# Moving factors and scan results of a state-space layer into PSUM, and writing out the order of its steps

## The chip, the core and the metric

The program runs on one core of one Trainium2 chip. Five engines take instructions from queues of their own, each in order: TensorE (PE, the matmuls), VectorE (DVE), ScalarE (ACT), GpSimd (POOL) and SyncE (SP, which here issues all large DMA transfers). An instruction that waits holds up everything behind it on its engine. The metric is the time of one execution on the device in microseconds (us), lower is better; of the kernel before three runs were taken.

## The reference

An encoder trunk of two layers works on one sequence of 512 positions and 1024 channels. Layer 0 mixes with dilated attention, layer 1 with a bidirectional state-space model (S5); each mixer is followed by a SwiGLU network (FFN 0 and FFN 1), and RMS norms stand ahead of all of them. The change lies in layer 1 and in its tables:

```python
def s5_direction(u, a_re, a_im, log_dt, b_re, b_im, c_re, c_im, reverse):
    dt = jnp.exp(log_dt)[:, None]
    mag = jnp.exp(a_re * dt)
    lr, li = mag * jnp.cos(a_im * dt), mag * jnp.sin(a_im * dt)
    ...
    bbr = fr[..., None] * b_re - fi[..., None] * b_im
    bbi = fr[..., None] * b_im + fi[..., None] * b_re
    bur = jnp.einsum('bsgc,gpc->bsgp', u, bbr)
    bui = jnp.einsum('bsgc,gpc->bsgp', u, bbi)
    ...
    _, _, xr, xi = lax.associative_scan(complex_affine_combine, (ar, ai, bur, bui),
                                        reverse=reverse, axis=1)
    return (jnp.einsum('bsgp,gcp->bsgc', xr, c_re) - jnp.einsum('bsgp,gcp->bsgc', xi, c_im))

def s5_mixer(hn, w_in, ..., d_skip, w_glu):
    u = (hn @ w_in).reshape(b, s, SSM_GROUPS, SSM_GROUP_CH)      # 64 groups of 16 channels
    y = d_skip * u + (s5_direction forward) + (s5_direction backward)
    ag = gelu(y) @ w_glu
    return ag[..., :D_MODEL] * sigmoid(ag[..., D_MODEL:])

def swiglu_ffn(hn, w_in, w_out):
    gu = hn @ w_in
    return (silu(gu[..., :FFN_HIDDEN]) * gu[..., FFN_HIDDEN:]) @ w_out
```

## The kernel before

Activations lie with channels on the partitions: a tile is 128 channels by 512 positions in fp32. A product is taken in three passes (high part by high part, low by high, high by low: `gemm_a`, the matmuls of L764), so one 128x512 result over 1024 channels costs 24 matmuls. For each unit of weights ScalarE writes the high part (`whi`, L116) and VectorE, in the SSM stage GpSimd, the low one (`wlo`, L117).

**Tables.** The scan is done in blocks of 8 positions. For each of 8 channel tiles T and each half s of its groups the class `Tables` computes from the parameters: `bb` (L212 to L217 from `elem_b`, VectorE), the input table `Tn` (`elem_in`, VectorE, L419 to L421, through a scratch tile `tm`), the output table `B` (`elem_out`, GpSimd), the phases `ph` (`elem_ph`, GpSimd, six doublings of a geometric series), and `Z` (`elem_z`, ScalarE, copies of `B` and `C`). TensorE then transposes `Tn` in two steps into `tps` (`tr_in`, L449) and multiplies `bb` by `Z` into `eps` (`band`, L458); ScalarE copies both results out (`Tt`, `E`), and DMAs put all tables into DRAM.

This work is cut into pieces that a planner (`Bg`) lays between the matmuls of FFN 0. Each piece has a cost; every k-tile of a product adds credit in proportion to its time, and the next piece is written into the program when the credit reaches half its cost. So the costs set places only: a piece's VectorE instructions stand in VectorE's queue where the program had got to. FFN 0 itself needs VectorE and ScalarE after each pair of products `gps` and `ups` (`evac`): `g` (L1171, VectorE), Silu (L1172, ScalarE), `u` (L1173) and `u*g` (L1175, VectorE), `hh` (L1178, ScalarE), `hl` (L1179, VectorE). Its results turn over five PSUM banks, the tables' over three.

**The SSM stage.** For each T: a product gives `sps` (24 matmuls), VectorE scales it into `u` (L1388), eight DMAs spread `u` by position into `U` (L1392), 64 small matmuls (L1281) give `V` (two banks, one set), `s_scan` turns `V` by the phases (L1299 to L1301), scans (L1306) and turns back (L1311 to L1313, result `xx`), `s_R` copies `xx` to `x` on ScalarE, half of it in reverse (L1323, L1325), 48 matmuls give `yps` (L1346, L1348), and ScalarE applies Gelu. Every second T the results are transposed (`s_tr`) and split for the GLU product. In the steady state the program of one T has: product T, `s_R` of T-3, V and scan of T-2, output of T-3. First halves of four GLU columns (`glu_part`, copied out by ScalarE at L1452) lie between the last steps.

## Time and profile before

| | us |
|---|---|
| median of 3 runs (1647.0 to 1652.1) | 1649.3 |
| profiled execution, its own time | 1651.6 |
| its span | 1649.6 |
| TensorE busy | 1538.5 (93%) |
| VectorE busy | 984.4 (60%) |
| ScalarE busy | 672.1 (41%) |
| GpSimd busy | 530.0 (32%) |

The span is what the trace covers; the execution's time is 2.0 us longer, and the profiled execution was 2.3 us above the median. TensorE is busy for 93% of the span, so what a change can win lies in the 111 us in which it is not, and in the time in which its clock is granted at less than full speed (the row PEclk, in tenths of full speed). FFN 0 lies from about 570 to 1030 us, the parameters' part of the tables in its first 110 us, the tables themselves from 690 on, the SSM stage from 1030 to 1210.

### The profile page before, as it was taken

To read this page: it belongs to the slowest core of one execution; us is meant where nothing else is said; L and a number is where in the kernel's file an instruction comes from. 1 tells how busy PE (TensorE), PEld (TensorE's weight loads), DVE (VectorE), ACT (ScalarE), POOL (GpSimd) and SP (SyncE) were. 2 spreads that over 40 slices of the span, in tenths; PEclk is the share of its full clock that TensorE was granted. 3 is DMA by queue.
4 is the path that set the end of the run, shared out by engine and by line. 5 is a ranking of instruction groups with operands and counts; after the bars stand their busy time and mean duration, and the time that the engine had idled before them with its cause. 6 is when DMAs were issued, how large, how long until landed. Compare 5 with 4: busy or idle time off the path is not lost. (4 is left out here: it accounts for less than half of the span.)

```text
span 1649.6 us, 22660 instructions
## 1 busy us (share of the span) xinstructions
PE 1538.5 (93%) x8428; PEld 1271.4 (77%) x8428; DVE 984.4 (60%) x1701; ACT 672.1 (41%) x1180; POOL 530.0 (32%) x790
## 2 busy tenths in 40 slices
PE   8999999999998899979979989987799999999997
PEld 6977887888896778767767767776678788888886
DVE  6366665666665588876777785567636533433233
ACT  5255454554464432434434443433333333332222
POOL 1022001011111240488889897445403111011010
PEclk9999999999999899999989998989899999999999
DMA  5321232232222133345655544657722333323332
GB/s 181 90 77 52 65 90 64 77 91 63 79 67 62 44 106 89 108 132 147 182 142 160 152 137 141 240 183 225 220 82 85 102 90 102 97 86 105 109 102 64
DMA packets 279180, 185.16 MB, mean 112 GB/s; under 512 B 39936, under 2 KB 261280, under 8 KB 277024
## 3 DMA queue, kind: packets, MB, share of 16 engines
q1 hardware_dynamic: 278640, 183.13, 37.3%
q8 instruction: 66, 1.08, 0.3%
q10 hardware_dynamic: 432, 0.60, 0.1%
q14 instruction: 42, 0.34, 0.1%
HBM read 154.34 MB, written 27.26 MB: 110 GB/s over the span
## 5 line engine op out<-in xcount | busy, mean ns | idle before, releaser
L117 DVE TENSOR_TENSOR wlo<-wraw,whi 128x1024 fp32r<-128x1024 f32 (+1 forms) x232 | 300.3, 1297 | 184.4 <-ACT whi L116 182.1
L116 ACT ACTIVATE whi<-wraw 128x1024 fp32r<-128x1024 f32 x238 | 241.3, 1018 | 247.9 <-PE ops L1572 73.4
L764 PE MATMUL gps<-xhi,whi 128*128 128x512 f32 x792 | 320.4, 405 | 0.0
L764 PE MATMUL gps<-xhi,wlo 128*128 128x512 f32 x792 | 311.4, 393 | 0.9 <-DVE wlo L117 0.9
L764 PE MATMUL gps<-xlo,whi 128*128 128x512 f32 x792 | 311.2, 393 | 0.5 <-DVE xlo L624 0.5
L958 POOL COPY st<-st 32x4 f32<-32x4 f32 x256 | 59.7, 233 | 457.5 <-ACT P L946 337.9
L764 PEld LDWEIGHTS gps<-xhi,wlo 128*128 128x128 f32 x792 | 149.8, 189 | 34.3 <-DVE wlo L117 1.3
L764 PEld LDWEIGHTS gps<-xhi,whi 128*128 128x128 f32 x792 | 150.0, 189 | 28.5 <-issue 2.5
L764 PEld LDWEIGHTS gps<-xlo,whi 128*128 128x128 f32 x792 | 150.3, 190 | 26.4 <-DVE xlo L624 0.8
L764 PE MATMUL ups<-xhi,wlo 128*128 128x512 f32 x352 | 139.6, 397 | 2.0 <-DVE wlo L117 2.0
L764 PE MATMUL ups<-xhi,whi 128*128 128x512 f32 x352 | 140.9, 400 | 0.0
L764 PE MATMUL ups<-xlo,whi 128*128 128x512 f32 x352 | 139.1, 395 | 0.0
L1175 POOL TENSOR_TENSOR u<-u,g 128x512 f32<-128x512 f32 x22 | 28.4, 1291 | 211.3 <-DVE u L1173 202.2
L946 ACT ACTIVATE P<-P,st 128x256 f32<-128x256 f32 x128 | 63.8, 499 | 70.3 <-DVE st L943 70.1
L1172 ACT ACTIVATE g<-g 128x512 f32<-128x512 f32 x44 | 27.8, 632 | 129.9 <-DVE g L1171 129.9
L764 PEld LDWEIGHTS ups<-xhi,wlo 128*128 128x128 f32 x352 | 67.2, 191 | 17.2 <-DVE wlo L117 2.8
L764 PEld LDWEIGHTS ups<-xhi,whi 128*128 128x128 f32 x352 | 67.3, 191 | 14.9 <-issue 1.5
L764 PEld LDWEIGHTS ups<-xlo,whi 128*128 128x128 f32 x352 | 67.2, 191 | 13.6
L866 PE MATMUL vps<-whi,xhi 128*128 128x256 f32 x256 | 73.3, 287 | 0.0
L764 PE MATMUL fps<-hh,whi 128*128 128x512 f32 x176 | 72.7, 413 | 0.0
L1178 ACT ACTIVATE hh<-u 128x512 fp32r<-128x512 f32 x44 | 27.8, 633 | 109.9 <-POOL u L1175 87.4
L866 PE MATMUL vps<-whi,xlo 128*128 128x256 f32 x256 | 72.4, 283 | 0.0
(321 smaller groups left out, 3262.9 us busy)
## 6 DMA issues: line engine op xcount, KB each, us to landing
wraw<-in_w_ffn_in SPq DMA_DIRECT2D x88, 512.0 KB, 3.8
wraw<-in_w_qkv SPq DMA_DIRECT2D x72, 512.0 KB, 3.6
wraw<-in_w_ffn_out SPq DMA_DIRECT2D x38, 512.0 KB, 4.0
BD<-B SPq DMA_DIRECT2D x16, 512.0 KB, 3.5
TinD<-Tt SPq DMA_DIRECT2D x16, 512.0 KB, 2.6
Ti<-TinD SPq DMA_DIRECT2D x8, 1024.0 KB, 6.0
Bt<-BD SPq DMA_DIRECT2D x8, 1024.0 KB, 6.3
wraw<-in_w_attn_out SPq DMA_DIRECT2D x8, 512.0 KB, 3.8
```

Source lines behind the costliest of these rows:

```text
L116: nc.scalar.activation(out=hv, in_=wv, func=ACTF.Copy)
L117: self.lo_engine.tensor_tensor(out=lv, in0=wv, in1=fv(hv), op=ALU.subtract)
L764: nc.tensor.matmul(dst, w[:, kt, :], x, start=(start and kt == ks[0] and j == 0), stop=(stop and kt == ks[-1] and j == 2))
L866: nc.tensor.matmul(ps[rp][:, r % 2, :], x, w[:, kk, :], start=(kt == 0 and j == 0 and r % 2 == 0), stop=(kt == 7 and j == 2 and r % 2 == 1))
L946: nc.scalar.activation(out=Pt[:, j, :], in_=Pt[:, j, :], func=ACTF.Exp, bias=st[:, 32 + off + j:33 + off + j], accum_out=st[:, 8 + off + j ...
L958: nc.gpsimd.tensor_copy(par[32 * z:32 * z + 32, y, :, :], own[32 * y:32 * y + 32, z, :, :])
L1172: nc.scalar.activation(out=g, in_=g, func=ACTF.Silu)
L1175: eng.tensor_tensor(out=u, in0=u, in1=g, op=ALU.mult)
L1178: nc.scalar.activation(out=hi, in_=u, func=ACTF.Copy)
```

## The change

**Tables.** `bb` and the scratch tile `tm` move from SBUF into PSUM (`pbb`, `ptm`, one bank each); a ScalarE copy of `bb` stays in SBUF for TensorE (`bbs`). The banks come from FFN 0's results (five to four) and the tables' results (three to two). The phases become products of two tables of 8 entries, prepared with the parameters (`AB`): six GpSimd operations of 128x512 for each T in place of 36 smaller ones and two memsets. The sign that ScalarE applied to `B` moves into the parameters. `Tn` and `B` get two buffers, and `band` and `tr_in` of a half-table run while the next half-table's elements are under way (`behind`). The planner's costs fall from 528,900 to 384,750 ns in sum, so its ratio to the 321.7 us of FFN 0 goes from 1.68 to 1.22.

**SSM stage.** There are two sets of V banks. `s_scan` is split into `s_pre`, which writes the scans' results back into V's banks, and `s_post`, which reads them there. Transposes go in halves through a bank of half the size, with a copy back to SBUF. The order of all steps is written out in one list, and the first halves of GLU columns (`fill`) are cut in two. The number of matmuls is the same (7696).

```diff
-        bb = self.bb[:, :, 0:128].rearrange("p i (g c) -> p i g c", g=8)
+        self.bbP = bb = self.pbb.tile([P, 2, 8, 16], F32, tag="bb", name="bbP")
         self.cmul(V, bb[:, 0], bb[:, 1], bt[:, 0], bt[:, 1], *f, self.t("bbT", [8, 16]))
+        nc.scalar.activation(out=self.bbs[T % 2][:, :, 0:128], in_=bb.rearrange("p i g c -> p i (g c)"), func=ACTF.Copy)
...
-        t, o = self.t("tm", [4, 8, 16]), self.Tn[:, i]
+        t, o = self.ptm.tile([P, 4, 8, 16], F32, tag="tm", name="tm"), self.Tn[T, s][:, i]
         tt(out=o, in0=self.bc(self.pin, 0, g0), in1=self.ch(bb[:, i]), op=ALU.mult)
         tt(out=t, in0=self.bc(self.pin, 1, g0), in1=self.ch(bb[:, 1 - i]), op=ALU.mult)
         tt(out=o, in0=o, in1=t, op=(ALU.subtract, ALU.add)[i])
...
+        sh = [P, 8, 8, 8]
+        lo = [self.AB[:, j, :, 0, 8 * T:8 * T + 8].rearrange("p k (g o) -> p g o k", o=1).to_broadcast(sh) for j in range(2)]
+        hi = [self.AB[:, j, :, 1, 8 * T:8 * T + 8].rearrange("p k (g o) -> p g k o", o=1).to_broadcast(sh) for j in range(2)]
...
+        tt(out=o, in0=hi[0], in1=lo[i], op=ALU.mult)
+        tt(out=t, in0=hi[1], in1=lo[1 - i], op=ALU.mult)
+        tt(out=o, in0=o, in1=t, op=(ALU.subtract, ALU.add)[i])
...
-        if i == 1:
-            nc.scalar.activation(out=B[:, 1], in_=B[:, 1], func=ACTF.Copy, scale=-1.0)
...
-        r = [(3400, lambda i=i: some(i)) for i in range(0, len(ops), n)]
+        r = [(1750, lambda i=i: some(i)) for i in range(0, len(ops), n)]
...
+                behind = [(1600, lambda T=T, s=s: self.band(T, s)), (400, lambda T=T, s=s: self.store_e(T, s)),
+                          (1600, lambda T=T, s=s: self.tr_in(T, s, 0)), (1600, lambda T=T, s=s: self.tr_in(T, s, 1)),
+                          (400, lambda T=T, s=s: self.store_in(T, s))]
...
-                psf = Cycle(((psg, "g"),) * 2 + ((f0.enter_context(tc.tile_pool(name="psf", bufs=3, space=PSUM)), "f"),) * 3)
-                psb = f0.enter_context(tc.tile_pool(name="psb", bufs=3, space=PSUM))
+                psf = Cycle(((psg, "g"),) * 2 + ((f0.enter_context(tc.tile_pool(name="psf", bufs=2, space=PSUM)), "f"),) * 2)
+                psb = f0.enter_context(tc.tile_pool(name="psb", bufs=2, space=PSUM))
+                tabs.ptm = f0.enter_context(tc.tile_pool(name="ptm", bufs=1, space=PSUM))
+                tabs.pbb = f0.enter_context(tc.tile_pool(name="pbb", bufs=1, space=PSUM))
...
-        pV = s0.enter_context(tc.tile_pool(name="psV", bufs=1, space=PSUM))
-        pY = s0.enter_context(tc.tile_pool(name="psY", bufs=2, space=PSUM))
+        pV = s0.enter_context(tc.tile_pool(name="psV", bufs=2, space=PSUM))
+        pY = s0.enter_context(tc.tile_pool(name="psY", bufs=1, space=PSUM))
...
-            for i in range(2):
-                q = W[i]
-                nc.vector.tensor_tensor_scan(out=q, data0=rho, data1=W[i], initial=0.0, op0=ALU.mult, op1=ALU.add)
-                Q.append(q)
+            for q, w in zip((Vr, Vi), W):
+                nc.vector.tensor_tensor_scan(out=q, data0=rho, data1=w, initial=0.0, op0=ALU.mult, op1=ALU.add)
+
+        def s_post(T):
...
+            Q = [vt[T][:, i].rearrange("p g j -> p (g j)") for i in range(2)]
...
+        def s_tr(t2, half):
...
+            for l in range(4):
+                nc.tensor.transpose(yt[:, l], y[:, l], ident)
+            nc.scalar.activation(out=y, in_=yt, func=ACTF.Copy)
+            if half == 1:
...
+        run((s_su, 2), (s_move, 2), (s_g, 3, 0), (s_V, 0), (s_g, 3, 1), (s_su, 3), (s_post, 0), (s_V, 1), (s_g, 4),
+            (s_ph, 0), (s_R, 0), (s_O, 0), (s_su, 4), (s_post, 1), (s_V, 2),
+            (s_g, 5, 0), (s_ph, 1), (s_g, 5, 1), (s_R, 1), (s_O, 1), (s_su, 5), (s_post, 2), (s_V, 3),
+            (s_tr, 0, 0), (s_ph, 2), (s_g, 6, 0), (s_tr, 0, 1), (s_R, 2), (s_post, 3), (s_g, 6, 1), (s_su, 6), (s_V, 4),
+            (s_O, 2), (s_ph, 3), (s_R, 3), (s_post, 4), (s_g, 7, 0), (s_O, 3), (s_g, 7, 1), (s_su, 7), (s_V, 5),
+            (s_tr, 1, 0), (s_ph, 4), (s_tr, 1, 1), (s_R, 4), (s_O, 4), (s_post, 5), (s_V, 6),
+            (next, fill[0]), (s_ph, 5), (next, fill[0]), (s_R, 5), (s_O, 5), (s_post, 6), (s_V, 7), (s_tr, 2, 0),
+            (next, fill[1]), (s_tr, 2, 1), (s_R, 6), (s_post, 7), (next, fill[1]), (s_O, 6), (next, fill[2]), (next, fill[2]))
         ws.lo_engine = nc.vector
-        glu_part(LATE[3])
...
+        run((s_R, 7), (s_O, 7), (next, fill[3]), (s_tr, 3, 0), (next, fill[3]), (s_tr, 3, 1))
```

What this does to the queues is seen at three places. First VectorE around the second half-table of a T, before. `Tn` of the first line is made in two threes (real and imaginary part), `g` to `hl` are the `evac` of one pair of products, `E` the end of the band before.

```order
L463 SCALAR_TENSOR_TENSOR E_6599<-cst_66,dcol_5495,E_6599 128x16
L419 TENSOR_TENSOR Tn_6633<-pin_5565,bb_6378 128x512
L420 TENSOR_TENSOR tm_6634<-pin_5565,bb_6378 128x512
L421 TENSOR_TENSOR Tn_6633<-Tn_6633,tm_6634 128x512
L1171 TENSOR_TENSOR g_6638<-gps2_6532,rsB2_5860 128x512
L1173 TENSOR_TENSOR u_6639<-ups_6576,rsB2_5860 128x512
L1175 TENSOR_TENSOR u_6639<-u_6639,g_6638 128x512
L1179 TENSOR_TENSOR hl_6645<-u_6639,hh_6644 128x512
L117 TENSOR_TENSOR wlo_6652<-wraw_6577,whi_6651 128x1024
L419 TENSOR_TENSOR Tn_6633<-pin_5565,bb_6378 128x512
L420 TENSOR_TENSOR tm_6661<-pin_5565,bb_6378 128x512
L421 TENSOR_TENSOR Tn_6633<-Tn_6633,tm_6661 128x512
```

After, at the corresponding place: the second three of a `Tn`, then the next T's `bb` in PSUM, then an `evac`.

```order
L440 TENSOR_TENSOR Tn_6535<-pin_5566,bbP_6327 128x512
L441 TENSOR_TENSOR tm_6556<-pin_5566,bbP_6327 128x512
L442 TENSOR_TENSOR Tn_6535<-Tn_6535,tm_6556 128x512
L213 TENSOR_TENSOR bbP_6581<-bt_6350,ff_5565 128x128
L214 TENSOR_TENSOR bbT_6582<-bt_6350,ff_5565 128x128
L215 TENSOR_TENSOR bbP_6581<-bbP_6581,bbT_6582 128x128
L216 TENSOR_TENSOR bbP_6581<-bt_6350,ff_5565 128x128
L217 TENSOR_TENSOR bbT_6582<-bt_6350,ff_5565 128x128
L218 TENSOR_TENSOR bbP_6581<-bbP_6581,bbT_6582 128x128
L1195 TENSOR_TENSOR g_6593<-gps2_6486,rsB2_5870 128x512
L1197 TENSOR_TENSOR u_6594<-ups_6540,rsB2_5870 128x512
L1199 TENSOR_TENSOR u_6594<-u_6594,g_6593 128x512
```

The second three of `Tn` stood behind a whole `evac` and a `wlo` before; now it stands ahead of the `evac`, which has the three and six `bb` operations in front of it. The transposes of this `Tn` come only after the following band.

Second, ScalarE at the same places, before: `Z` is filled behind the `evac`'s Silu (`g`), `hh` and `whi`, and the sign of `B` between its two parts.

```order
L461 ACTIVATE E_6599<-eps_6590 128x240
L1172 ACTIVATE g_6638<-g_6638 128x512
L1178 ACTIVATE hh_6644<-u_6639 128x512
L116 ACTIVATE whi_6651<-wraw_6577 128x1024
L438 ACTIVATE Z_6376<-B_6616 64x4x112
L439 ACTIVATE Z_6376<-B_6616 64x4x112
L440 ACTIVATE Z_6376<-C_6383 128x4x16
L116 ACTIVATE whi_6710<-wraw_6649 128x1024
L436 ACTIVATE B_6616<-B_6616 128x512
L438 ACTIVATE Z_6376<-B_6616 64x4x112
L439 ACTIVATE Z_6376<-B_6616 64x4x112
L440 ACTIVATE Z_6376<-C_6383 128x4x16
```

After: copies of `C` and of `bb` come first, then Silu, `hh` and `whi`, then both parts of `Z`.

```order
L116 ACTIVATE whi_6543<-wraw_6487 128x1024
L401 ACTIVATE C_6579<-cps_6576 128x256
L431 ACTIVATE bb1_6319<-bbP_6581 128x2x128
L1196 ACTIVATE g_6593<-g_6593 128x512
L1202 ACTIVATE hh_6599<-u_6594 128x512
L116 ACTIVATE whi_6606<-wraw_6541 128x1024
L459 ACTIVATE Z_6316<-B_6453 64x4x112
L460 ACTIVATE Z_6316<-B_6453 64x4x112
L461 ACTIVATE Z_6316<-C_6325 128x4x16
L459 ACTIVATE Z_6316<-B_6453 64x4x112
L460 ACTIVATE Z_6316<-B_6453 64x4x112
L461 ACTIVATE Z_6316<-C_6325 128x4x16
```

The copy `bb1` waits for VectorE's `bb`, the Silu for VectorE's `g`, and all of `Z`, for which TensorE's next instruction of the tables (`eps`) waits, stands behind both. In the program of before the transposes `tps` came between `Z` and `eps`.

Third, VectorE in the SSM stage, from the turn of one V to the turn of the next, before.

```order
L1299 TENSOR_TENSOR t1_9943<-V_9910,ph_9489 128x512
L1300 TENSOR_TENSOR t2_9944<-V_9910,ph_9489 128x512
L1299 TENSOR_TENSOR t1_9948<-V_9910,ph_9489 128x512
L1300 TENSOR_TENSOR t2_9949<-V_9910,ph_9489 128x512
L1306 SCALAR_TENSOR_TENSOR t1_9943<-rr0_9756,t1_9943 128x512
L1306 SCALAR_TENSOR_TENSOR t1_9948<-rr0_9756,t1_9948 128x512
L1311 TENSOR_TENSOR xx_9955<-t1_9943,ph_9489 128x512
L1312 TENSOR_TENSOR t2_9956<-t1_9948,ph_9489 128x512
L1311 TENSOR_TENSOR xx_9960<-t1_9948,ph_9489 128x512
L1312 TENSOR_TENSOR t2_9961<-t1_9943,ph_9489 128x512
L1388 TENSOR_TENSOR u_10004<-sps2_9967,rsB2_9851 128x512
L1299 TENSOR_TENSOR t1_10040<-V_10007,ph_9609 128x512
```

After, the same stretch: the scans write to `V`, and the scaled `u` of the next product stands between them and the turn back.

```order
L1322 TENSOR_TENSOR t1_9701<-V_9666,ph_9224 128x512
L1323 TENSOR_TENSOR t2_9702<-V_9666,ph_9224 128x512
L1322 TENSOR_TENSOR t1_9706<-V_9666,ph_9224 128x512
L1323 TENSOR_TENSOR t2_9707<-V_9666,ph_9224 128x512
L1327 SCALAR_TENSOR_TENSOR V_9666<-rr0_9493,t1_9701 128x512
L1327 SCALAR_TENSOR_TENSOR V_9666<-rr0_9493,t1_9706 128x512
L1423 TENSOR_TENSOR u_9725<-sps2_9652,rsB2_9588 128x512
L1338 TENSOR_TENSOR xx_9727<-V_9666,ph_9224 128x512
L1339 TENSOR_TENSOR t2_9728<-V_9666,ph_9224 128x512
L1338 TENSOR_TENSOR xx_9732<-V_9666,ph_9224 128x512
L1339 TENSOR_TENSOR t2_9733<-V_9666,ph_9224 128x512
L1322 TENSOR_TENSOR t1_9773<-V_9738,ph_9344 128x512
```

The count is the same; operands move from `t1` (SBUF) to `V` (PSUM), and one `u` goes ahead of the turn back.

## Rows read from the trace of the kernel before

**Rows 1.** Stages: length, busy us of PE, PEld, DVE, ACT, POOL, clock, DMA share, GB/s.

```profile
570.00:690.00 120.00, 115.14 (x510) 93.55 (x509) 102.24 (x198) 38.62 (x49) 30.30 (x23) 1.00 0.36 96
690.00:1030.00 340.00, 301.05 (x1485) 233.70 (x1484) 249.89 (x283) 145.98 (x255) 291.94 (x402) 0.94 0.52 149
1030.00:1078.00 48.00, 43.31 (x196) 34.92 (x194) 23.14 (x37) 21.72 (x21) 19.29 (x11) 1.00 0.64 220
1078.00:1210.00 132.00, 107.28 (x1163) 90.06 (x1163) 83.81 (x93) 47.70 (x70) 62.92 (x40) 0.90 0.65 202
```

**Rows 2.** TensorE's waits, 690 to 1030 us: total, times, longest.

```profile
PE tps L449 <- DVE Tn L421: 38.2, 16, 6.4
PE eps L458 <- ACT Z L440: 0.7, 2, 0.5
```

**Rows 3.** TensorE's waits, 1078 to 1210 us.

```profile
PE yps L1348 <- ACT x L1325: 15.0, 11, 4.8
PE pe L764 <- ACT gpart L1452: 8.9, 1, 8.9
PE V L1281 <- DMA U<-u: 3.5, 1, 3.5
```

**Rows 4.** A matmul's price, from the chain that ended last: start, us, 528 matmuls.

```profile
1521.26 119.69 PE ops L1572 x528
```

**Rows 5.** Groups of VectorE, 690 to 1030 us: count, busy us, mean ns, idle before.

```profile
L420 DVE TENSOR_TENSOR tm<-pin,bb 128x512 f32<-128x512 f32 x32 | 33.4, 1044 | 0.0
L419 DVE TENSOR_TENSOR Tn<-pin,bb 128x512 f32<-128x512 f32 x31 | 28.8, 931 | 0.0
L421 DVE TENSOR_TENSOR Tn<-Tn,tm 128x512 f32<-128x512 f32 x32 | 27.1, 846 | 1.1
```

**Rows 6.** Timeline at 980 us, steps of one evac: start, us, instruction.

```profile
980.10 0.68 DVE L1171 TENSOR_TENSOR g<-gps,rsB 128x512 f32<-128x512 f32 x1
...
980.81 0.63 ACT L1172 ACTIVATE g<-g 128x512 f32<-128x512 f32 x1 [9.26 <-DVE g L1171]
...
981.47 0.74 DVE L1175 TENSOR_TENSOR u<-u,g 128x512 f32<-128x512 f32 x1
...
982.24 0.63 ACT L1178 ACTIVATE hh<-u 128x512 fp32r<-128x512 f32 x1 [0.81 <-DVE u L1175]
```

**Rows 7.** GpSimd's work on the phases (tile ph), 690 to 1030 us.

```profile
690.00:1030.00 340.00, 154.59 (x304) 0.94 0.52 149
```

**Rows 8.** Timeline of the SSM stage, 1104 to 1106 us.

```profile
1104.31 2.08 PE L1281 MATMUL V<-U,Ti 128*64 128x64 f32 x64
...
1104.42 1.28 POOL L1313 TENSOR_TENSOR xx<-xx,t 128x512 f32<-128x512 f32 x1 [0.72 <-PE sps L764]
...
1105.73 0.63 ACT L1323 ACTIVATE x<-xx 64x512 f32<-64x512 f32 x1 [0.72 <-POOL xx L1313]
```

**Rows 9.** Groups of ScalarE, 690 to 1030 us.

```profile
L116 ACT ACTIVATE whi<-wraw 128x1024 fp32r<-128x1024 f32 x40 | 42.0, 1051 | 27.6 <-DMA wraw<-in_w_ffn_in 16.1 <-PE gps L764 6.1 <-PE fps L764 2.8
...
L439 ACT ACTIVATE Z<-B 64x448 f32<-64x448 f32 x31 | 17.8, 575 | 0.4
...
L1172 ACT ACTIVATE g<-g 128x512 f32<-128x512 f32 x15 | 9.5, 632 | 58.5 <-DVE g L1171 58.5
L440 ACT ACTIVATE Z<-C 128x64 f32<-128x64 f32 x31 | 8.0, 257 | 0.5
```

**Rows 10.** VectorE in the parameters' part: their helper's line L178, then everything.

```profile
575.00:680.00 105.00, 34.32 (x114) 1.00 0.36 100
...
575.00:680.00 105.00, 89.12 (x185) 1.00 0.36 100
```

**Rows 11.** Groups of VectorE, 1078 to 1210 us.

```profile
L1306 DVE TENSOR_TENSOR_SCAN t<-rr,t 128x512 f32<-128x512 f32 x16 | 26.8, 1712 | 9.7 <-ACT rr L1287 5.1 <-POOL t L1301 4.6
...
L1299 DVE TENSOR_TENSOR t<-V,ph 128x512 f32<-128x512 f32 x16 | 10.9, 683 | 19.0 <-DMA ph<-PhD 14.8 <-PE V L1281 4.2
...
L1311 DVE TENSOR_TENSOR xx<-t,ph 128x512 f32<-128x512 f32 x16 | 10.7, 669 | 0.0
```

More of the change, by code (lines that the diff above doesn't have):

```diff
@@ L245, in sincos @@
         V = self.V
[L246 removed]
+        sc = [self.scratch(f"sc{i}", 512) for i in range(4)]
+        k_, r, y2, p = (t[:, 0:448] for t in sc)
         two_pi = 2.0 * np.pi
@@ L1384, in build, with s_V, s_O, s_ph @@
+        def s_V(T):
+            s_rho(T)
+            for g in range(8):
+                s_v(T, g)
+            if T + 2 < KT:
+                load_tab(T + 2, "Ti")
+            s_pre(T)
+        def s_O(T):
+            for q in range(4):
+                s_out(T, q)
+            s_gelu(T)
+            if T + 3 < KT:
+                s_move(T + 3)
+            if T + 2 < KT:
+                load_tab(T + 2, "Mt", "Bt")
+        def s_ph(T):
+            load_tab(T + 2, "ph")
         us = {}
```

302 lines of the change are left out of this document (123 added, 179 removed).

## Prediction

> **What bounds the kernel now.** I read the busy time by stage first, then TensorE's waits in the two stages that the change touches, then the groups of VectorE and ScalarE there. The reader is to see in the stages [rows 1] that TensorE sets the time but loses some of it in two places. From 690 to 1030 us, where the tables are built under FFN 0, it is idle for 340 - 301.05 = 39.0 us, and the granted clock is 0.94 of full speed: 0.06 x 340 = 20.4 us at most. From 1078 to 1210 us, the SSM stage, it is idle for 24.7 us, and the clock of 0.90 costs at most 13.2 us. In the stretches between them, where TensorE is busy for 90% or more, the clock is 1.00 [rows 1]; so I read the low clock as what follows the waits, and let its loss go with them in proportion.
>
> The waits have names. In the table stage 38.2 of the 39 us are transposes `tps` that wait for VectorE's `Tn`, 16 times, once for each half-table, and `eps` waits for hardly anything, 0.7 us [rows 2]. In the SSM stage `yps` waits 15.0 us for ScalarE's copies `x`, a GLU product 8.9 us for its bank to be copied out, V 3.5 us for the DMAs into U [rows 3]; with 0.2 us of small ones 27.6 us. The number of matmuls does not change, so nothing else can be won, and about 97 us (39 + 20.4 + 24.7 + 13.2) bounds the gain.
>
> A unit for what follows: 528 matmuls took 119.69 us [rows 4], 0.227 us each. A product over 1024 channels (24) is 5.44 us, a pair of products 10.9 us.
>
> **Table stage, the wait that goes.** From the order and 0.227 us a matmul, `Tn`'s second three stood 5.4 us of TensorE's time ahead of its transposes before, mostly behind a whole `evac`; now it is 9.3 to 11.7 us, because `band` and other pieces come between. The waits of before were 2.4 us in the mean and 6.4 at most [rows 2], and 4 to 6 us more cover them nearly all. I leave 3 us of 38.2.
>
> VectorE gets lighter too. The three operations of `Tn` take 931, 1044 and 846 ns [rows 5]; `g`, as large but with an operand in PSUM, takes 0.68 us [rows 6]. If all three come down to that, 32 x (2.82 - 2.04) = 25 us of VectorE's 249.9 go; if the move to PSUM does nothing, none. No row shows VectorE writing to PSUM; the nearest rows lie at 0.68 (reading it) and 1.04 us, and I take 0.7 to 0.8. GpSimd's phases, 154.6 us in 304 instructions [rows 7], become 48 of 128x512, each about 1.28 us by the nearest row [rows 8], or 61 us. GpSimd isn't waited for, so this counts only by freeing VectorE.
>
> Here a rule of the Trainium skill can be set beside the rows ("SBUF — State Buffer", section "Who interferes with whom"): a VectorE instruction with two SBUF inputs takes an interface that GpSimd's reads share, one with a single SBUF input doesn't. The trace agrees as far as it goes, 0.68 us against 0.85 to 1.04. By it all of `Tn` would run at 0.68 us whatever GpSimd does, but the products in `bb`, with both inputs in SBUF, would be held up as before; the next step's wait would then be nearer to its lower figure, and the sum, with 8 us of waits less and the clock's share, some 12 us lower, 1584.
>
> **Table stage, the wait that comes.** `eps` needs both parts of `Z`, and now it comes 2.8 us of TensorE's time after the second part is issued, with nothing else of the tables between. On ScalarE `Z` stands behind Silu, `hh` and `whi` of an `evac`, and Silu waits for VectorE's `g`, behind `Tn` and the six `bb`. From the end of a pair of products: `g` 0.68, Silu 0.63, `u*g` 0.74, `hh` 0.63 [rows 6], `whi` 1.05, twice (2 x 0.575 + 0.257) for `Z` [rows 9]; 3.7 us to the end of `whi`, 6.5 to that of `Z`. If the end of the pair falls evenly over the 10.9 us ahead of `eps`, and VectorE is on time, the mean wait is 0.36 us: 1.2 us in the 2.2 us in which it falls between the parts of Z, 0.8 in the 1.6 us before. If VectorE is 2 us late it is 1.2 us, if it is 4.2 us late (58.5/14, Silu's mean wait in [rows 9]) 2.6 us. Only 15 pairs, 163 of the 301 us, lie in the stage; the rest are products without `evac`. So 8.7 of the 16 half-tables pay: 3, 11 or 23 us. I take 11, since VectorE has nine operations (6 or 7 us) just ahead of some `g` and none ahead of others.
>
> Banks: with two for `tps`, `eps` and `cps`, the third in a row needs ScalarE's copy of the first. Where an `evac` lies between, I count 0.7 us, four times: 3 us. With four banks for the results a pair's bank is wanted again 10.9 us after it was full, more than the 9.26 us that Silu waited in the rows at 980 us [rows 6], so I put that at nothing; its price if VectorE is later than that is the excess. The sign of `B` that leaves ScalarE and the copy of `bb` that comes there balance.
>
> Waits: 3 + 11 + 3 = 17 in place of 38.9 us, 22 saved; the clock's 20.4 shrink to 20.4 x 17/38.9 = 8.9, 11.5 saved.
>
> **The parameters.** 114 instructions of the helper's line took 34.3 us, 0.30 each [rows 10]; 134 take 40. By the order the first `cps` stands 13 us of TensorE's time earlier, 92 in place of 105 us; the other 54.8 us of VectorE's work there scale to 48, so VectorE is busy for 88 of 92 us. I charge 3 us of waits (0 to 6). The table part gains 22 + 11.5 - 3 = 30 us, between 12 (`eps` at 23) and 43 (`eps` at 3).
>
> **SSM stage.** From V's last matmul the turn takes four products at 0.68, an addition of 1.28 on GpSimd and two scans at 1.7 [rows 8, 11], with the first addition beside the products 6 to 7 us; the turn back, the addition and the copies at 0.63 that the first output matmuls need, 5 more. That is 11 to 12 us. Before, the next product (5.4) and V itself, in the one set of banks, lay in between. In the new order TensorE has, between V of T and its output: 10.2 us for T = 0 (2.7 + V 2.0 + 5.4), 14 to 19 for T = 1 to 3, about 14 for T = 4, 6 and 7, 11 for T = 5. So output 0 waits 0.9, outputs 1 to 3 nothing. The later ones have the time, but ScalarE's queue brings others ahead of `x`: the half-transposes' copies and the high parts, which wait for transposes just ahead of the output (T = 4 and 6: 3.2 and 1.7 us), and copies of `gpart` (T = 5 and 7: 2.3 each). V 0 and 1 still wait 1.6 of the 3.5 us for U. Together 12.0 in place of 27.6 us: 15.6 saved, and of the clock's 13.2 the share 7.5. The scans that write to PSUM have no row; by the nearest, products that read it (683 ns beside 669 from SBUF [rows 11]), nothing is lost; if each of 16 took one more product's time, 0.68 us, most of the 11 us would fall under TensorE's work, and I keep 8 as the bad end. The SSM part gains 23 us, 8 to 33.
>
> **Sum.** 30 + 23 = 53 us. The profiled execution took 1651.6 us, 2.3 above the median of 1649.3, so it would come to 1598.6 and the median to 1596 us.
>
> **Rivals.** (a) The new waits don't come: three waits of some 2 us are left in each stage, and the clock is back at 1.00. Table part 34 + 20 - 3 = 51, SSM part 23 + 13 = 36; 87 us, 1562. For it: the stretches with 96% busy run at full clock [rows 1]. Against it: two queues that have to be on time at once.
>
> (b) The wait only changes its name: VectorE stays as late as it was, since `bb` still reads SBUF, and `eps` pays what `tps` paid. The table part loses its 3 us, SSM gains 23: 1629. For it: VectorE is busy for 249.9 of 340 us [rows 1], and the pairs of products hold more than their share of that.
>
> (c) The transfers take the SSM gain. DMA is busy for 0.65 of 132 us there [rows 1], 86 us, which would be 79% of a stage of 109 us. VectorE waited 14.8 us for `ph` [rows 11]; if that comes onto TensorE's path, SSM keeps 8 us: 38 in all, 1611.
>
> (d) Slower: `eps` takes over the whole of Silu's mean wait in every half-table, 16 x 4.2 = 67 us, with 6 of the others 73 in place of 38.9; the clock follows (+18) and the 3 us, so the tables lose 55, SSM gains 23: 32 slower, 1681. It decides from 3.3 us a half-table on, where the loss is 23. For it: ScalarE's copies of Z have the last place in both queues. Against: half of the half-tables see no `evac`.
>
> **Chances.** The forecast 0.52 (its own range 1576 to 1622), (a) 0.15, (b) 0.11, (c) 0.13, (d) 0.09, of which a third ends within 0.3%, about what a measurement of this kernel can tell from no change. So faster 0.91, same 0.03, slower 0.06. The range of 1558 to 1638 takes in (a) to (c) and leaves out (d) and what lies below (a).
>
> **What would show it.** In the profile after, TensorE's waits from 690 to 1030 us should name `eps` and ScalarE's `Z` with 5 to 20 us and `tps` with under 5; the three operations of `Tn` should take 0.7 to 0.8 us; the clock should be about 0.97 there. In the SSM stage `yps` should wait under 12 us and the GLU product for nothing. It would be wrong if `tps` still waited over 15 us, if new waits for a result bank (`gps`, `ups`) turned up, or if the time came from stretches outside 570 to 1210 us.

## The result

The change makes the kernel slower: 1668.2 us (median of 4 runs, 1662.6 to 1671.3) against 1648.2 us of the kernel before on the same chip (median of 4), a ratio of 1.012 [1.010, 1.014]. The forecast was 1596 us with a range of 1558 to 1638, so it failed in sign and size. The best version of the study keeps the table part and turns two of its steps round: 1618.2 us, a ratio of 0.981 [0.979, 0.983].

### The profile page after: what moved, and what is told of

Same layout as the page of the kernel before. It is cut to its first block, busy times and chain, and to the rows that moved or that the text cites. A ratio compares the mean times of both kernels' runs of the same rounds, so it can differ in the third digit from the quotient of the medians.

```text
span 1669.0 us, 22457 instructions
## 1 busy us (share of the span) xinstructions
PE 1546.2 (93%) x8428; PEld 1273.9 (76%) x8428; DVE 977.7 (59%) x1721; ACT 667.6 (40%) x1180; POOL 449.9 (27%) x535
## 5 line engine op out<-in xcount | busy, mean ns | idle before, releaser
L117 DVE TENSOR_TENSOR wlo<-wraw,whi 128x1024 fp32r<-128x1024 f32 (+1 forms) x232 | 310.9, 1342 | 203.1 <-ACT whi L116 199.7
L452 POOL TENSOR_TENSOR B<-pout,C 128x512 f32<-128x512 f32 x32 | 42.3, 1323 | 155.8 <-DVE pout L178 63.6
L786 PEld LDWEIGHTS ups<-xhi,whi 128*128 128x128 f32 x352 | 66.4, 189 | 14.8 <-issue 1.9
L888 PE MATMUL vps<-wlo,xhi 128*128 128x256 f32 x256 | 72.5, 283 | 0.0
L888 PE MATMUL vps<-whi,xlo 128*128 128x256 f32 x256 | 72.5, 283 | 0.0
```

Source lines behind the costliest of these rows:

```text
L117: self.lo_engine.tensor_tensor(out=lv, in0=wv, in1=fv(hv), op=ALU.subtract)
L452: tt(out=B[:, i], in0=self.bc(self.pout, i, g0), in1=self.ch(C[:, 0]), op=ALU.mult)
L786: nc.tensor.matmul(dst, w[:, kt, :], x, start=(start and kt == ks[0] and j == 0), stop=(stop and kt == ks[-1] and j == 2))
L888: nc.tensor.matmul(ps[rp][:, r % 2, :], x, w[:, kk, :], start=(kt == 0 and j == 0 and r % 2 == 0), stop=(kt == 7 and j == 2 and r % 2 == 1))
```

## The profile after

The profiled execution took 1671.3 us with a span of 1669.0, 19.4 us more than the span before. The first place to look is where these microseconds lie. The table takes them from the first and last matmul of each name in the two traces. 48 matmuls of `pe`, early parts of GLU products, moved from the SSM stage to the GLU columns; their 48 x 0.227 = 10.9 us [rows 4] are counted in both stretches, before and after alike. By its matmuls FFN 0 lies from 595.7 to 1055.9 us before, a little later than the stages suggest.

| stretch | before, us | after, us | difference | forecast |
|---|---|---|---|---|
| FFN 0 with the tables (first `gps` to last `fps`) | 460.2 | 447.3 | -12.9 | -30 |
| SSM stage (to the first `pg`, new order + 10.9) | 161.0 | 165.9 | +4.9 | -23 |
| GLU columns (`pg`, as 288 matmuls) | 65.5 | 93.0 | +27.5 | 0 |

Three differences of -12.9, +4.9 and +27.5 make +19.5, as much as the 19.4 of the spans; what lies ahead of FFN 0 and behind the columns differs by a few us each way and cancels. One trace fixes the first two only to several us. In the seven kernels of the study whose FFN 0 is the changed one it took 447.3 to 454.8 us, in the three with the old one 457.1 to 460.2, so the tables gained some 8 us there. The new SSM order took 162.5 to 167.6 us in five kernels that share it, and these two ends are kernels that differ only behind it. The columns took 93.0 and 93.4 us in the two kernels that have them in this form. So each part has its own answer, and the largest stands where the prediction had not looked. First, the stages, in the columns of [rows 1], after, and the GLU columns before:

```profile
570.00:690.00 120.00, 106.98 (x466) 84.58 (x464) 100.54 (x209) 33.52 (x43) 29.95 (x26) 1.00 0.31 85
690.00:1030.00 340.00, 315.13 (x1582) 244.65 (x1582) 245.04 (x296) 146.18 (x259) 213.44 (x147) 0.97 0.57 163
1078.00:1210.00 132.00, 104.59 (x1026) 87.53 (x1025) 82.87 (x90) 55.93 (x82) 58.79 (x37) 0.88 0.62 202
1210.00:1285.00 75.00, 61.72 (x239) 49.40 (x238) 34.81 (x35) 17.51 (x22) 14.23 (x11) 0.89 0.25 71
```

```profile
1210.00:1285.00 75.00, 72.51 (x324) 59.55 (x322) 47.58 (x48) 26.11 (x32) 19.61 (x15) 1.00 0.29 84
```

In the table stage TensorE is idle for 24.9 instead of 39.0 us, where 17 were forecast; its clock is 0.97 instead of 0.94, as forecast. But from 570 to 690 it is idle for 13.0 instead of 4.9 us, in the SSM window for 27.4 instead of 24.7, and in the GLU columns, where before it was busy for 72.5 of 75 us at full clock, for 13.3 us at a clock of 0.89.

TensorE's waits over the whole span after, as in [rows 2, 3] (total, times, longest):

```profile
PE eps L479 <- ACT Z L461: 21.5, 16, 4.8
PE pg L786 <- DVE gpart L1493: 17.6, 4, 4.7
PE yps L1375 <- ACT x L1352: 14.5, 10, 4.2
PE V L1305 <- DMA U<-u: 8.1, 2, 5.9
PE eps L479 <- POOL tm L413: 7.4, 1, 7.4
```

`tps` is gone from the list (38.2 us before). `eps` takes 28.9 us in its place, `yps` stays near what it was, V waits for U more than twice as long, and a wait of 17.6 us is new: the GLU product `pg` waits for VectorE's addition. Here is one of its four cases, on VectorE and on TensorE (start, us, instruction):

```profile
1249.05 2.20 DVE L117 TENSOR_TENSOR wlo<-wraw,whi 128x1024 fp32r<-128x1024 f32 x1
1251.17 0.68 DVE L1493 TENSOR_TENSOR gpart<-pg,gpart 128x512 f32<-128x512 f32 x1
```

```profile
1251.90 0.50 PE L786 MATMUL pg<-yh,whi 128*128 128x512 f32 x1 [3.95 <-DVE gpart L1493]
...
1252.99 0.63 PE L786 MATMUL pg<-yh,whi 128*128 128x512 f32 x1
1253.42 0.63 PE L786 MATMUL pg<-yl,whi 128*128 128x512 f32 x1
...
1256.35 0.40 PE L786 MATMUL pg<-yh,whi 128*128 128x512 f32 x1
1256.59 0.39 PE L786 MATMUL pg<-yl,whi 128*128 128x512 f32 x1
```

The change does this in lines that the cuts shown above leave out:

```diff
+            pp = pV.tile([P, 2, 8, 64], F32, tag="V", name="pg").rearrange("p i g j -> p i (g j)")
+            pp = [pp[:, i] for i in range(2)]
...
-                    ps = (pY, p1)[part].tile([P, S], F32, tag="yf"[part], name="pg")
```

Both halves of a column now lie in one tile of two banks of V's set, and the addition of the first half is written between the two products. The second product writes to the same tile, so the program makes its first matmul wait for that addition, which stands behind a `wlo` of 2.2 us on VectorE. After the 3.95 us without work the matmuls start 0.43 us apart, which is the clock's lower level (1.2 GHz; the granted clock of 1251 to 1256 us is 0.66), and from 1255.88 on 0.24 us apart again (2.4 GHz). Before, the addition was written at the same place, but each half had a tile of its own, so nothing waited for it, and both additions ran back to back behind both products:

```profile
1255.69 1.27 DVE L1495 TENSOR_TENSOR gpart<-pg,gpart 128x512 f32<-128x512 f32 x2
```

## Experiments

All ratios are to the kernel before on the same chip, with a 95% interval.

### 1. Where the loss lies: the additions, the table part, the SSM part

**GLU additions behind both products** (changed kernel):

```diff
                 for part in range(2):
                     gemm_a(Yl[4:], pp[part], ...)
+                for part in range(2):
                     t = parts.pop((m, part))
```

> The changed kernel with one edit: in the last four GLU columns both halves' products are issued before the two additions, not each addition right behind its product. Theory (the second product waits for the addition of the first, because both write one two-bank tile): the four waits of 17.6 us on the addition go, and with them the low clock of that stretch (8.6 us); 1668 - 26 = 1642 us. Rival A (only the waits go, the low clock has another cause): 1668 - 18 = 1650 us. Rival B (the wait is for a bank set that is still in use from the column two before): nothing changes, 1668 us.

Measured: 1649.5 us, 0.9998 [0.998, 1.0015]. The columns take 65.6 us at full clock: the whole 27.5 us are gone from them. About 20 came back in all, since 7.4 turned up at the first product of FFN 1, which wants the banks of V's set in which the last column lies:

```profile
PE gps L786 <- DVE gpart L1494: 7.4, 1, 7.4
```

**The kernel before with the table part alone**, that is, all edits ahead of the SSM stage:

```diff
+        self.bbP = bb = self.pbb.tile([P, 2, 8, 16], F32, tag="bb", name="bbP")
...
+                tabs.pbb = f0.enter_context(tc.tile_pool(name="pbb", bufs=1, space=PSUM))
```

> The kernel before with the table part of the change alone (class of tables, planner costs, banks under FFN 0); SSM stage and GLU as before. Theory (the parts add up; between the same matmuls the tables gained 29 us after the first half of FFN 0's hidden columns and lost 17 in it): 1648 - 12 = 1636 us. Rival A (as predicted, 30 us gain): 1618 us. Rival B (the gain is lost again in the SSM stage, whose transfers start at another time): 1648 us.

Measured: 1638.8 us, 0.993 [0.990, 0.996].

**The kernel before with the SSM and GLU part alone:**

```diff
+        pV = s0.enter_context(tc.tile_pool(name="psV", bufs=2, space=PSUM))
...
+        run((s_su, 2), (s_move, 2), (s_g, 3, 0), (s_V, 0), ...
```

> The kernel before with the SSM and GLU part of the change alone, the tables as before. Theory: the stage from the last product of FFN 0 to the end of the GLU columns took 32 us longer in the changed kernel, whatever the tables do: 1648 + 32 = 1680 us. Rival A (the loss comes from the tables' new schedule, which leaves transfers behind): 1648 us or less. Rival B (as predicted): 1625 us.

Measured: 1678.6 us, 1.017 [1.014, 1.020].

**The same with the additions behind both products** (first diff):

> The same kernel with the additions of the last four GLU columns behind both products. Theory: 26 us of the 32 are the GLU columns, the SSM steps themselves lose some 5: 1653 us. Rival (the written-out order gains its 23 us once the GLU columns no longer hide it): 1625 us.

Measured: 1658.1 us, 1.005 [1.004, 1.007]. The additions are worth 20.5 us here, and the same 7.4 us are left at FFN 1. The parts add up: 0.7% gained by the tables and 1.7% lost by the rest make 1.0% lost, 1.2% measured. What remains of the SSM order without its GLU columns is worth nothing, not 23 us.

### 2. The tables: who holds `Z`

**ScalarE's copy of `bb` behind `Z`** (table part alone):

```diff
-        nc.scalar.activation(out=self.bbs[T % 2][:, :, 0:128], in_=bb...)
...
+                if s == 1 and T + 1 < KT:
+                    u.append((0, self.copy_b))
```

> The table part alone, with ScalarE's copy of bb moved behind both parts of Z in its queue (where the next T's factors are made). Theory (that copy waits for VectorE, 41.3 us in 6 waits, and holds up Z, for which TensorE waits): the waits of eps in the half-tables behind a bb, some 13 of 26 us, go, with a share of the low clock; 1639 - 15 = 1624 us. Rival (Z is held up as much by the Silu in front of it, which waits for the same VectorE queue): unchanged, 1639 us.

Measured: 1623.3 us, 0.986 [0.984, 0.988].

**An empty piece of 16,000 ns in the planner ahead of the first tables** (table part alone):

```diff
+        r.append((16000, lambda: None))
         r.append((1000, lambda: (self.elem_C(0), self.elem_b(0))))
```

> The table part alone, with an empty piece of 16000 ns cost ahead of the first table, so that the first factors stand 13 us of matmul time later, about where they stood before. Theory (the loss in the first half of the hidden columns is VectorE and GpSimd being late with the parameters at the start): the first wait of eps, 7.3 us, goes; 1639 - 8 = 1631 us. Rival (the loss is in waits of every half-table, and the pause packs the rest 4% closer): 1639 us or a little more.

Measured: 1633.6 us, 0.992 [0.990, 0.994], within the interval of the table part alone. In the trace the first wait of `eps` falls from 7.3 to 3.5 us and FFN 0 from 448.2 to 443.3 us, no more than traces of one FFN 0 differ by.

**`Z` ahead of the next T's `bb`** (table part alone):

```diff
+                u += [(2600, lambda T=T, s=s: self.elem_z(T, s, 0)), (2600, lambda T=T, s=s: self.elem_z(T, s, 1))]
                 if s == 1 and T + 1 < KT:
                     u.append((1500, lambda T=T: (self.elem_C(T + 1), self.elem_b(T + 1))))
-                u += [(2600, lambda T=T, s=s: self.elem_z(T, s, 0)), (2600, lambda T=T, s=s: self.elem_z(T, s, 1))]
```

> The table part alone, with Z's two pieces placed ahead of the next T's factors bb in the planner's list (VectorE's bb then stands behind, not between Tn and the evac of the products). Theory (Z is held up by the copy of bb and by the Silu whose g stands behind bb): the eps waits shrink by as much as with the copy moved, and by the second wait of 6.5 us too; 1623 - 5 = 1618 us. Rival (bb then comes late for the next Tn, and tps waits instead): 1625 us or more.

Measured: 1618.2 us, 0.981 [0.979, 0.983], the best of the study. TensorE's waits for the tables in the table part alone, and with `Z` first:

```profile
PE eps L479 <- ACT Z L461: 18.7, 16, 4.6
PE eps L479 <- POOL tm L413: 7.3, 1, 7.3
```

```profile
PE eps L479 <- POOL tm L413: 7.4, 1, 7.4
PE eps L479 <- ACT Z L461: 4.6, 7, 1.2
...
PE tps L470 <- ACT E L482: 2.4, 2, 1.8
```

The wait for `Z` falls by 14 us, and FFN 0 with the tables takes 429.7 us, 30.5 less than before. That is the gain the prediction had put on the table part.

**The same with an empty piece of 10,000 ns** (as above):

> The same with an empty piece of 10000 ns ahead of the first table. Theory (the first eps still waits 7 us for GpSimd, whose output table waits for VectorE's last parameters): 1618 - 6 = 1612 us. Rival (the pause only moves the wait, as in the run with the pause alone): 1618 us.

Measured: 1621.1 us, 0.984 [0.981, 0.986]. The first wait stays (8.6 us, now on GpSimd's `B`).

### 3. The SSM stage: what is late at `yps`

**Low parts of the weights on VectorE** (changed kernel with the additions behind, as the next three):

```diff
-        ws.lo_engine = nc.gpsimd
+        ws.lo_engine = nc.vector
```

> The changed kernel with the GLU additions behind both products, and with the low parts of the weights made on VectorE, not on GpSimd, in the SSM stage. Theory (five of 16 scans take 3.1 to 3.6 us in place of 1.2, each beside one of GpSimd's low parts, and hold up the outputs' inputs): the scans' total falls from 38.7 to 28 us, 11 low parts of 1.2 us come to VectorE, and the waits of yps fall from 16.6 to about 10; 1649 - 6 = 1643 us. Rival A (the scans are not on the path, the transfers are): 1649 us. Rival B (the low parts in VectorE's queue wait for ScalarE and hold up the turns): 1655 us.

Measured: 1653.0 us, 1.002 [1.000, 1.004]. The sixteen scans get shorter as expected, 28.2 us in sum instead of 36.3, but the stage does not (164.3 instead of 164.8 us), so they are not what it waits for.

**Weight loads issued behind U and `ph`:**

```diff
+                ws.la = 2 if T in (5, 6, 7) else 3
...
+        def s_ld():
+            ws.la = 3
+            ws.load_to(ws.n + 2)
```

> The changed kernel with the GLU additions behind both products, and with the first three loads of GLU weights (8 DMAs each) issued behind the moves into U and the loads of the phases, not ahead of them. Theory (SyncE's queue: the weights' DMAs wait for earlier large transfers and hold up U and ph behind them): the waits of V for U fall from 7.8 to 2 us and VectorE's waits for ph from 27 to about 15, the SSM stage is 9 us shorter; 1640 us. Rival (the transfers themselves are slow, or the weights are late instead): 1649 us or more.

Measured: 1653.6 us, 1.004 [1.002, 1.006]. V's wait for U goes, and two others pay:

```profile
PE yps L1375 <- ACT x L1352: 22.4, 11, 8.9
PE yt L1388 <- ACT ys L1380: 7.2, 1, 7.2
```

**Weight loads of the GLU product from GpSimd's queue:**

```diff
-                    nc.sync.dma_start(
+                    nc.gpsimd.dma_start(
```

> The changed kernel with the GLU additions behind both products, and with the split loads of GLU weights (8 DMAs a unit) issued from GpSimd's queue instead of SyncE's. Theory (SyncE's queue bounds the SSM stage: eight moves into U take it 6 to 9 us, eight loads of weights 6, tables 2, some 16 us for each of 8 T, as long as the stage itself): with the weights gone from it, V's waits for U (7.8 us) and VectorE's for ph (27 us) mostly go, and the stage is 10 to 15 us shorter; 1649 - 12 = 1637 us. Rival A (the transfers, not their issue, are the limit): 1649 us. Rival B (issuing costs GpSimd so much that the additions of the turns come late): 1655 us or more.

Measured: 1648.9 us, 1.000 [0.998, 1.002].

**The moves into U from T = 3 on out of GpSimd's queue:**

```diff
-                nc.sync.dma_start(out=Us[T % 3]...
+                (nc.gpsimd if T > 2 else nc.sync).dma_start(out=Us[T % 3]...
```

> The changed kernel with the GLU additions behind both products, and with the moves into U of T = 3 to 7 (40 DMAs) issued from GpSimd's queue. Theory (SyncE's queue bounds the stage): as in the run with the weights, but the moves stand in GpSimd's order between the turns' additions; 1649 - 10 = 1639 us. Rival A (the transfers are the limit): 1649 us. Rival B (GpSimd's queue, waiting for the output of T before the moves, holds up the turns): 1655 us or more.

Measured: 1645.8 us, 0.998 [0.996, 1.000]. VectorE's wait for `ph` falls from 26.6 to 3.3 us, `yps` still waits 15.4.

**The GLU weights from GpSimd's queue in the old order** (table part with the copy behind `Z`; the diff is that of two runs above):

> The table part with ScalarE's copy of bb behind Z, the SSM stage of before, and the split loads of GLU weights issued from GpSimd's queue. Theory (the 9 us that a GLU product waits are really a weight load that lands late because SyncE issued it late; ScalarE stands idle for 14 us before that unit's high part): that wait goes; 1623 - 10 = 1613 us. Rival A (it is the copy of gpart that is late): 1623 us. Rival B (issuing costs GpSimd too much): 1630 us or more.

Measured: 1636.6 us, 0.992 [0.990, 0.994], some 11 us worse by the ratios than without it: VectorE's scans now wait 18.9 us for GpSimd's additions, behind the issues on its queue.

**All repairs on the changed kernel** (additions, copy of `bb` behind `Z`, and the last GLU column in banks outside V's set):

```diff
+            if m == KT - 1:
+                pp = [pY.tile([P, S], F32, tag="y", name="pg"), pT.tile([P, S], F32, tag="yt", name="pg")]
```

> The changed kernel with three edits: the GLU additions behind both products, the last GLU column's products in two banks outside V's, ScalarE's copy of bb behind Z. Theory (the next product after the GLU columns waits 7.4 us because its banks are those of V's sets, still being read): that wait goes, and 12 to 13 us of the tables as in the run of the tables alone; 1649 - 7 - 12 = 1630 us. Rival (FFN 1's first product waits for the last column's own chain anyway): 1637 us.

Measured: 1628.8 us, 0.987 [0.985, 0.990]. The 7.4 us at FFN 1 are gone.

**The same without the loads of the phases from T = 2 on** (this run and the next leave out transfers that the result needs, so they only price them):

```diff
-            load_tab(T + 2, "ph")
+            ld[T + 2]["ph"] = ld[T % 2]["ph"]
```

> The changed kernel with the three edits, and with the phases of T = 2 to 7 not loaded in the SSM stage (the tables of T = 0 and 1 are used in their place, so six transfers of 512 KB and VectorE's waits for them are left out of the computation). Theory A (VectorE's 25 us of waits for the phases make the turn of V late, 23 us from V to the copies in place of the 11 to 12 predicted): yps waits fall from 16 to under 8 us, the stage is 8 to 12 us shorter; 1629 - 10 = 1619 us. Theory B (ScalarE's queue makes the copies late whatever VectorE does): 1629 us.

Measured: 1618.9 us, 0.983 [0.981, 0.986].

**Also without the moves into U from T = 3 on:**

```diff
-            if T + 3 < KT:
-                s_move(T + 3)
```

> The same, and also without the moves into U for T = 3 to 7 (40 DMAs; old U is used). Theory A (SyncE's queue and the transfers behind it are what the written-out order runs into): V's waits of 7 us go too, and the stage comes near the predicted order, some 20 us shorter than with both: 1629 - 19 = 1610 us. Theory B (ScalarE's queue): at most the 7 us of U, 1622 us.

Measured: 1613.0 us, 0.979 [0.977, 0.981]. By the ratios the two kinds of transfers cost 7 and 8 us, each within some 5. TensorE's wait here, without either:

```profile
PE yps L1381 <- ACT x L1358: 14.5, 11, 3.4
```

**All repairs, `Z` first, phases loaded from GpSimd's queue** (behind its last addition of the same T; nothing is left out):

```diff
-                nc.sync.dma_start(out=t, in_=src)
+                (nc.gpsimd if n == "ph" and T > 1 else nc.sync).dma_start(out=t, in_=src)
```

> The changed kernel with the GLU additions behind both products, the last GLU column in two banks outside V's, Z ahead of the next factors, and the phases of T = 2 to 7 issued from GpSimd's queue right behind the last addition that uses the old ones (nothing is left out). Theory (the phases come late because SyncE reaches them late, not because the transfer is long): VectorE's waits for them go from 25 to under 8 us, 8 of the 10 us that leaving them out gave; 1623 - 8 = 1615 us. Rival (the transfer itself, shared with the tables' and the weights', is what takes the time): 1623 us.

Measured: 1622.9 us, 0.986 [0.984, 0.987]. VectorE no longer waits for `ph`, but V waits 9.0 us for U and `yps` 12.6.

**The best version with the same edit:**

> The table part with Z ahead of the next factors, the SSM stage of before, and the phases of T = 2 to 7 issued from GpSimd's queue behind the last addition that uses the old ones. Theory: VectorE waited 14.8 us for the phases there too; about half of it comes to TensorE: 1618 - 5 = 1613 us. Rival (TensorE's waits there are for other things, the transfers only shift): 1618 us.

Measured: 1618.9 us, 0.983 [0.982, 0.985]: no difference to the best version, although VectorE's 14.2 us of waits for the phases are gone.

## Why the prediction was wrong

**The step that was missing: the GLU columns.** The prediction priced the tables and the SSM stage and named 570 to 1210 us as the place of the change; "the GLU product for nothing" was said of its bank only. The diff gave the pair of banks of V's set to the GLU columns, and the order of the addition and the second product made a wait of it. It is shown: moving two additions behind both products takes 20 us away in two kernels (1668.2 to 1649.5, 1678.6 to 1658.1), and the 7.4 us at FFN 1 are gone in the run that took the last column out of V's banks. With the additions moved the change is even with the kernel before, and without the 7.4 us it would be some 0.5% faster (an estimate, 1649.5 - 7.4 = 1642), not 50 us.

**Table stage, the wait that goes: right.** `tps` kept nothing (3 us forecast). `Tn` took 0.68 to 0.69 us, just under the 0.7 to 0.8 taken for it, beside [rows 5]:

```profile
L441 DVE TENSOR_TENSOR tm<-pin,bbP 128x512 f32<-128x512 f32 x32 | 22.0, 687 | 0.0
L442 DVE TENSOR_TENSOR Tn<-Tn,tm 128x512 f32<-128x512 f32 x32 | 22.0, 686 | 1.1
L440 DVE TENSOR_TENSOR Tn<-pin,bbP 128x512 f32<-128x512 f32 x32 | 21.7, 679 | 0.0
```

**Table stage, the wait that comes: mis-sized, 11 us forecast (14 with the banks), 21.5 found, and 7.4 more at the first `eps`.** The step that failed is the sentence that the sign of `B`, which leaves ScalarE, and the copy of `bb`, which comes there, balance. They were weighed as work. The groups of ScalarE from 690 to 1030 us (columns of [rows 9]) say more, the sign before and the copy after:

```profile
L436 ACT ACTIVATE B<-B 128x512 f32<-128x512 f32 x16 | 9.9, 619 | 6.8 <-POOL B L217 4.7 <-POOL ph L389 2.2
```

```profile
L431 ACT ACTIVATE bb<-bbP 128x256 f32<-128x256 f32 x7 | 2.7, 383 | 41.3 <-DVE bbP L218 41.3
```

The work falls by 7.2 us, but the copy waits for VectorE for 41.3 us where the sign waited for 6.8. ScalarE's waits there, after:

```profile
ACT bb L431 <- DVE bbP L218: 41.3, 6, 9.2
ACT g L1196 <- DVE g L1195: 32.1, 7, 6.3
```

Silu's wait fell from 58.5 to 32.1 us, and 41.3 us of a new one stand ahead of it, 6.9 us each time, with Silu, `hh`, `whi` and all of `Z` behind. I had worked out the mean wait of `eps` with VectorE 2 to 4 us late. By the ratios, putting the copy behind `Z` gave 12 us, putting `Z` ahead of `bb` altogether 19.

**The parameters: 3 us forecast, about 4 found, and 7.4 not forecast.** The idle time from 570 to 690 us rose by 8.2 us, 4.2 of it the beginning of the first `eps`'s wait. The list of waits names GpSimd's `tm` for that wait, but `eps` started at 693.15, just where ScalarE had finished the first `Z`, while `B` was ready at 688.6. ScalarE, and the last step of `B` on GpSimd:

```profile
686.67 0.38 ACT L431 ACTIVATE bb<-bbP 128x256 f32<-128x256 f32 x1 [12.47 <-DVE bbP L218]
687.26 0.63 ACT L1196 ACTIVATE g<-g 128x512 f32<-128x512 f32 x1 [0.21 <-DVE g L1195]
...
689.72 1.99 ACT L116 ACTIVATE whi<-wraw 128x1024 fp32r<-128x1024 f32 x2
...
692.80 0.26 ACT L461 ACTIVATE Z<-C 128x64 f32<-128x64 f32 x1
```

```profile
687.34 1.26 POOL L454 TENSOR_TENSOR B<-B,tm 128x512 f32<-128x512 f32 x1
```

It is the queue of the forecast once more: the copy of the first `bb` waits 12.5 us for VectorE, which is still at the parameters, and Silu, `hh` and two `whi` follow it ahead of `Z`. By the program the tables start 13 us of TensorE's time earlier, but the parameters on VectorE do not. Of the two empty pieces in the plan one shortened this wait (3.5 us) and one did not (8.6), and neither made the kernel faster beyond the noise; neither moved this copy alone, so what would is open.

**SSM stage: 23 us forecast, nothing found.** The 8.9 us of the GLU product that waited for its bank are gone, as forecast. But `yps`, which was to keep 10.4 us, waits for 17.2, and V's wait for U is 8.1 instead of 1.6. The step that failed is the chain from V to the copies, "11 to 12 us". From the end of V's last matmul to the last copy of `x` it took 16.4 to 25.9 us for the eight T, 22.9 in the mean. The trace of before had shown that a chain of this kind is longer than its work: 12.3 to 29.6 us there, 19.2 in the mean. Of the 22.9 us 5.2 are VectorE's, which starts the turn late, and 2.8 are finished `xx` that wait for ScalarE. The rest is work, 14.9 us, and also more than was added up, since a pair of scans took 4.9 us where 3.4 were taken. I had left out three waits. One stretch shows all three, on TensorE, VectorE, GpSimd and ScalarE:

```profile
1135.65 3.19 PE L1305 MATMUL V<-U,Ti 128*64 128x64 f32 x64 [2.22 <-DMA U<-u]
1138.77 1.09 PE L1388 MATMUL yt<-cst,ys 128*128 128x128 f32 x4
```

```profile
1143.88 0.69 DVE L1322 TENSOR_TENSOR t<-V,ph 128x512 f32<-128x512 f32 x1 [6.92 <-DMA ph<-PhD]
```

```profile
1135.34 2.51 POOL L1340 TENSOR_TENSOR xx<-xx,t 128x512 f32<-128x512 f32 x2 [3.99 <-DVE t L1339]
```

```profile
1139.95 0.60 ACT L1389 ACTIVATE ys<-yt 128x512 f32<-128x512 f32 x1 [8.06 <-PE yt L1388]
...
1142.98 0.61 ACT L1350 ACTIVATE x<-xx 64x512 f32<-64x512 f32 x1
```

V of T = 5 is finished at 1138.8, but its turn starts at 1143.9, because the phases land late: 5 us. The result `xx` of T = 4 is finished at 1137.9 and copied from 1143.0 on, 5 us late, because ScalarE stands at the copies of a half-transpose, which TensorE reaches only behind V 5, and V 5 had waited 2.2 us for U. So the new list ties three engines together: a late U holds TensorE, TensorE holds ScalarE, ScalarE holds `yps`. (The list puts a wait of `yps` here, 2.7 us, down to a weight load, but it ends at 1144.29, just behind ScalarE's second copy; with it `yps` waits 17.2 us, not 14.5.)

The transfers are late at their issue. SyncE's queue ahead of this stretch (each row lasts as long as the queue was at these issues):

```profile
1117.03 10.94 SPq L88 DMA_DIRECT2D wraw<-in_w_glu  x8
1128.07 0.54 SPq L1248 DMA_DIRECT2D Ti<-TinD  x1
1128.70 5.34 SPq L1427 DMA_DIRECT2D U<-u  x8
...
1135.25 0.38 SPq L1248 DMA_DIRECT2D ph<-PhD  x1
```

U is issued behind eight weight loads that hold the queue for 10.9 us, and `ph` behind U, 3.5 us before V is finished; it lands 8.5 us later. With the moves into U on another queue VectorE waited 3.3 us for `ph`. VectorE's waits for `ph`, of [rows 11], grew with it, and so did the scans:

```profile
L1327 DVE TENSOR_TENSOR_SCAN V<-rr,t 128x512 f32<-128x512 f32 x16 | 38.7, 2417 | 2.5 <-POOL t L1324 1.7
L1322 DVE TENSOR_TENSOR t<-V,ph 128x512 f32<-128x512 f32 x16 | 11.0, 686 | 30.1 <-DMA ph<-PhD 27.1 <-PE V L1305 3.1
```

27.1 us instead of 14.8. This is rival (c), "the transfers take the SSM gain", and in mechanism it was the nearest: without `ph` the stage gets 7.4 us shorter in the trace, without U 8.5 more. But other orders and queues gained at most 4.6 us, less than the 5.1 by which two traces of the same order differ, since each made another thing late:

| SSM stage, counted as above | us | `yps` waits | V waits for U |
|---|---|---|---|
| before | 161.0 | 15.0 | 3.5 |
| changed kernel | 165.9 | 17.2 | 8.1 |
| additions behind | 164.8 | 16.6 | 7.8 |
| low parts on VectorE | 164.3 | 14.8 | 9.2 |
| weight loads behind U and `ph` | 168.2 | 22.4 | 0 |
| weight loads from GpSimd | 162.6 | 19.0 | 3.4 |
| moves into U from GpSimd | 160.2 | 15.4 | 6.0 |
| all repairs | 163.9 | 16.0 | 7.0 |
| all repairs, `Z` first, phases from GpSimd | 159.3 | 12.6 | 9.0 |
| all repairs, without `ph` | 156.5 | 12.6 | 6.9 |
| without `ph` and U | 148.0 | 14.5 | 0 |

Even without both kinds of transfers 13 of the 23 us are all that is won, and `yps` waits as long as ever. The traces show where the time goes. With all repairs VectorE starts the turn 4.8 us behind V in the mean and `xx` waits 2.5 us for ScalarE; without `ph` it is 0.6 and 5.4, so two thirds of what VectorE gained were lost at ScalarE, and the chain went from 22.1 to 20.9 us only. At T = 4 `xx` was ready at 1111.2 there, but its copy came at 1122.4, behind the same copies of a half-transpose:

```profile
1119.41 0.60 ACT L1395 ACTIVATE ys<-yt 128x512 f32<-128x512 f32 x1 [8.08 <-PE yt L1394]
```

That ScalarE's place in the list is the rest of the loss is still argued: no run moved `s_R` in the new list by itself.

**The rivals.** (b), "the wait only changes its name", was half right: the name changed from `tps` to `eps`, at 28.9 of 38.2 us. (d) had named the place, ScalarE's copies of `Z` last in both queues, but less than half of its 67 us came. Its turning point was put too high, 3.3 us a half-table for a loss of 23; with the 6 us of other waits that its own sum counts it is 2.9. The forecast gave 0.06 to slower. What it lacked was a case for an edit outside the two stages whose waits it had read: the statement of what would prove it wrong did name that, "if the time came from stretches outside 570 to 1210 us", but with no price.

## What to carry to other kernels

When a change gives results another tile, read for each tile of several banks, which read comes between two writes: an addition between two products into one tile cost 20 us, and writing it behind both brought them back. An instruction that moves to another engine's queue is to be priced with what it waits for there, not with its own 0.4 us. And a wait on TensorE may be the last of a ring of engines; moving the issue of one transfer mostly moved the wait to the next member, and only fewer transfers shortened the stage by more than the 5 us by which its traces differ.
